# A hybrid diffusion step on one core: attention's K, V and Q loads on ScalarE's DMA queue with third Q and gate buffers, and DRAM scratch laid out by chunk and by head

## The chip, the cores and the metric

The kernel runs on one core of a Trainium2 chip. The metric is device microseconds from launch to end. The program is one launch that computes two layers and the final norm.

## What is computed

The reference runs a backbone of two layers on 1024 latent tokens and 128 context tokens (model width 1024). Cut to what matters here, one layer is:

```python
u = rms_norm(x, norm1_g) * (1 + sc1) + sh1
(aq, ak, av), dl, ml, bg, co = prep_mixers(u, w_in, ...)      # one projection
a = diff_attention(rope(aq), concat(rope(ak), k_ctx), concat(av, v_ctx), lam)   # 4 heads, 2 maps each
o_d = delta_bidir(...)                                        # 4 heads, gated DeltaNet, both directions
h_m = mlstm_bidir(...)                                        # 4 heads, mLSTM, both directions
x = x + g1 * (concat(norm(a), norm(o_d)*silu(bg), sigmoid(co)*norm(h_m)) @ w_out)
x = x + g2 * swiglu(rms_norm(x, norm2_g) * (1 + sc2) + sh2)
```

Attention takes, per head, two softmax maps over nine tiles of 128 keys (eight latent, one cached) for latent queries and one tile for context queries, and subtracts the second map times lambda from the first.

## The kernel before

All data is float32; a dense product is split into high and low parts and takes three matmuls (`mm3`, L189 to L191). A layer has four stages: the input projection (w_in), in which column blocks of the projection are made and written to scratch in DRAM; the mixers (the rest of prep2, attention, and the two chunked recurrences with merge); the output projection (w_out); and the FFN. In the profiled execution layer 0's w_in ends at about 547 us and its mixers at about 950; layer 1's mixers run from about 2427 to 2830.

The scratch in DRAM is made by open_s (L411): BT (conv outputs q, k, v of DeltaNet, transposed), CQK (mLSTM's q and k), QD and KD (attention's q and k in two parts), VD (attention's values), BC (gates), ND and RD (DeltaNet's prepared chunks). Stores into it: blk_b L727 (BT), blk_c L746 (CQK), tok_cols L560 (BC) and L565 (VD), attn_consts L924 (cached values into VD). Loads out of it: prep1 L754 (`cv` from BT) and L756 (`c` from CQK), delta_step L1062 (`qk` from BT), mlstm_step L1149 (`cq` from CQK), merge L1188 (`bc` from BC).

prep2 works on a pair of chunks: it loads `w` from ND (L851), solves a triangular system with small matmuls (tile `px`, L879 to L909, 32x32 and 64x64), with copies on ScalarE between them (`X`, L861; `T6`, L864), and stores `X` to RD (L911). Some calls of prep2 are left when w_in ends, and run beside the first attention blocks.

attention (from L1215) loops over 4 heads. Per head it loads two K tiles (L1228, 640 KB each, read as 4 groups of 32 rows of 5120 B, pool of 3 buffers), one V tile (L1231, 640 KB, 2 buffers), and for each of five blocks of queries a Q tile in two DMAs (L1236, 2 buffers). Per 128 queries: scores `s` on TensorE (L1250), scaling and running maximum on VectorE (L1251), exp on ScalarE (L1256), the difference of the maps on VectorE and GpSimd, transposes (L1277), copies `wt` out of PSUM on ScalarE or VectorE (L1280), the product `o` with V (L1284), its square sum and scaling on ScalarE (L1287, L1292).

```python
k = self.t(at, [P, NT + P], "K", 3, F32R)
nc.sync.dma_start(k.bitcast(F32), S["KD"][h // 2].rearrange("l p r t -> (l p) r t")[:, r:r + 32, :])
V = self.t(at, [P, 10, 128], "V", 2)
nc.sync.dma_start(V, S["VD"][:, :, 128 * h:128 * h + 128].rearrange("s p e -> p s e"))
q = self.t(at, [P, 2, 2, 256], "Q", 2, F32R)
```

The order of instructions on each engine and DMA queue is set when the program is built: the scheduler simulates the program's engines and buffers and writes down one order for each. On the chip each engine runs its own order strictly, and a DMA that is issued by SyncE (SP) or ScalarE (ACT) is one instruction of that engine: if it has to wait, what stands behind it on that engine waits too. Beside the data it depends on, each DMA of these two queues waits for the completion semaphore that it takes (there are eight, DMAHW0 to DMAHW7, given out in turn), and so for the DMA that held it last.

Of the kernel before, what the change touches and what calls it, by code (L numbers as in the profile page):

```python
# [9 lines left out]
F32 = mybir.dt.float32  # L10
# [7 lines left out]
P = 128  # L18
# [52 lines left out]
class Kern:  # L71
# [362 lines left out]
    def open_s(self, l):  # L434

        S = self.S = {}
        dt = lambda n, shape: self.dr.tile(shape, F32, name=f"{n}{l}")
        S["BT"] = dt("BT", [P, 6, CVO])
        S["CQK"] = dt("CQK", [P, 4, NT])
        S["V1"] = dt("V1", [NCH, P, H, 65])  # L440
        S["BC"] = dt("BC", [NCH, P, 512])
        S["QD"] = dt("QD", [8, 2, 64, NT])
        S["KD"] = dt("KD", [2, 2, 2, P, NT + P])
        S["VD"] = dt("VD", [10, P, 512])
        S["ND"] = dt("ND", [2, NCH, P, H, P])
        S["RD"] = dt("RD", [2, NCH, P, 1024])
        S["GR"] = dt("GR", [2, 16, NT])
        S["VK"] = dt("VK", [NCH, P, 768])
        S["RM"] = dt("RM", [2, NCH, P, 768])
        S["CAT"] = dt("CAT", [KB, P, NT])  # L450
        ed, pe = ExitStack(), ExitStack()
        self.dn = ed.enter_context(self.pool("psdn", PSUM))
        self.pp = pe.enter_context(self.pool("pspp", PSUM))
        return ed, pe
# [69 lines left out]
    def tok_cols(self, l, u, i, pr):  # L524
# [17 lines left out]
        for tt in range(NCH):  # L542
# [13 lines left out]
            else:  # L556
# [8 lines left out]
                nc.sync.dma_start(S["VD"][tt if tt < 8 else 9, :, off:off + 256], v)  # L565
            yield

# [137 lines left out]
    def blk_b(self, l, b, u):  # L705
# [21 lines left out]
        nc.sync.dma_start(S["BT"][:, b, :], a)  # L727
# [8 lines left out]
    def blk_c(self, l, b, u):  # L736
        nc, S, pr = self.nc, self.S, self.pr
        w = self.load_w(self.A["w_st"][l, 6 + b])
        bias = self.p(l, "bst")[:, 6 + b:7 + b]
        for g in range(NG):  # L740
            ps = self.ps(self.dn, "dn", 2)
            self.block(ps[:, :GW], w, u[g])
            o = self.t(pr, [P, GW], "gw", GB)
            nc.scalar.activation(o, ps[:, :GW], AF.Identity, bias=bias)
            c = slice(GW * g, GW * g + GW)
            nc.sync.dma_start(S["CQK"][:, b, c], o)  # L746

    def prep1(self, l, c, c1):

        nc, S, pr, pp = self.nc, self.S, self.ch, self.pp  # L750
        o = slice(cpos(c), cpos(c) + 128)
        oc = slice(128 * c, 128 * c + 128)
        q6 = self.t(self.cv, [P, CVW], "cv", 4)[:, :768].rearrange("p (a t) -> p a t", t=128)
        nc.sync.dma_start(q6, S["BT"][:, :, o])  # L754
        c4 = self.t(c1, [P, 4, 128], "c4", 1)
        nc.sync.dma_start(c4, S["CQK"][:, :, oc])  # L756
# [157 lines left out]
    def attn_consts(self, l):  # L914
# [6 lines left out]
        for i in range(2):  # L921
            cv = self.t(pr, [P, GW], "gw", GB)[:, :256]
            nc.sync.dma_start(cv, A["cv"][l][:, 256 * i:256 * i + 256])
            nc.sync.dma_start(S["VD"][8, :, 256 * i:256 * i + 256], cv)  # L924
# [121 lines left out]
    def delta_step(self, l, cs, S0, S1, seen):  # L1046
# [12 lines left out]
        if S0 is not None:  # L1059
            qk = self.t(sc, [P, 2, 4, 128], "qk", 2)  # L1060
            for d in range(2):
                nc.sync.dma_start(qk[:, d], S["BT"][:, 0:4, cpos(cs[d]):cpos(cs[d]) + 128])  # L1062
# [63 lines left out]
    def mlstm_step(self, l, cs, C0, C1, seen):  # L1126
# [4 lines left out]
        for d in range(2):  # L1131
# [15 lines left out]
            if C0 is not None:  # L1147
                cq = self.t(sc, [P, 2, 128], "cq", 3)
                nc.sync.dma_start(cq, S["CQK"][:, 0:2, 128 * c:128 * c + 128])  # L1149
# [34 lines left out]
    def merge(self, l, c):  # L1184

        nc, S, sc, pz = self.nc, self.S, self.sc, self.pz
        bc = self.t(sc, [P, 512], "bc", 2)
# [23 lines left out]
    def attention(self, l):  # L1211
# [11 lines left out]
        for h in range(H):  # L1223
            K = []
            for m in range(2):
                k = self.t(at, [P, NT + P], "K", 3, F32R)
                r = 64 * (h % 2) + 32 * m
                nc.sync.dma_start(k.bitcast(F32), S["KD"][h // 2].rearrange("l p r t -> (l p) r t")[:, r:r + 32, :])  # L1228
                K.append(k)
            V = self.t(at, [P, 10, 128], "V", 2)  # L1230
            nc.sync.dma_start(V, S["VD"][:, :, 128 * h:128 * h + 128].rearrange("s p e -> p s e"))  # L1231
            for q0 in range(0, NT, 256):
                nq = min(256, NT - q0)
                q = self.t(at, [P, 2, 2, 256], "Q", 2, F32R)
                for hh in range(2):
                    nc.sync.dma_start(q[64 * hh:64 * hh + 64, :, :, :nq].bitcast(F32), S["QD"][2 * h:2 * h + 2, :, :, q0:q0 + nq].rearrange("m l p t -> p m l t"))  # L1236
# [317 lines left out]
```

## Time and profile before

| | us |
|---|---|
| median of 3 runs | 3792.27 (3789.85 to 3796.47) |
| profiled execution | 3797.68 |
| its span, first to last instruction | 3795.9 |
| TensorE busy | 3540.6 (93%) |
| VectorE busy | 2295.8 (60%) |
| ScalarE busy | 1136.6 (30%) |
| GpSimd busy | 654.4 (17%) |
| mean granted TensorE clock | 0.954 of full speed |

The page gives shares of busy time over the whole span. The views that follow it cut the span into stretches, list one engine's instructions in time order with what ended each idle time, and sum what an engine waited for. SPq and ACTq are the DMA-issuing instructions of SyncE and ScalarE: a long one is an issue that stood waiting.

### The profile page before, as it was taken

What the parts mean: (1) busy time and instruction counts of PE and PEld (TensorE: products, weight loads), DVE (VectorE), ACT (ScalarE), POOL (GpSimd) and SP (SyncE); (2) the same over time, 40 slices, a digit from 0 to 9 for tenths busy, and PEclk for the clock granted to TensorE, in tenths of its full rate; (3) what the DMA queues carried; (4) which work ended last, traced back from release to release, by engine and by line L of the source; (5) the groups of instructions that cost most, each with busy time, mean ns of one, the idle gap of its engine ahead of it and who ended that gap; (6) DMA issues with size and microseconds to landing.
All of it is one profiled execution on the core that took longest, in us unless ns stands there. A gap on an engine that the chain in (4) does not pass through costs nothing. (4 is left out here: it accounts for less than half of the span.)

```text
span 3795.9 us, 59415 instructions
## 1 busy us (share of the span) xinstructions
PE 3540.6 (93%) x22770; PEld 3369.8 (89%) x22770; DVE 2295.8 (60%) x5361; ACT 1136.6 (30%) x2383; POOL 654.4 (17%) x903
## 2 busy tenths in 40 slices
PE   7999978997899999999999997898789999999998
PEld 6997777886899999999989877788778999999997
DVE  7896677787455566654485567477775434333435
ACT  5323315445241111111243431244553311111111
POOL 2014232355020000000020324034632000000001
PEclk8999988999999999999999999889999999999999
DMA  5377624774212222221133663467542111111111
GB/s 215 128 247 234 217 78 124 225 214 132 92 59 84 78 81 81 95 78 48 59 110 99 221 230 97 132 175 205 137 140 66 34 39 41 49 40 39 51 45 56
DMA packets 277091, 434.13 MB, mean 114 GB/s; under 512 B 24648, under 2 KB 186504, under 8 KB 276552
## 3 DMA queue, kind: packets, MB, share of 16 engines
q1 hardware_dynamic: 247576, 324.29, 27.3%
q10 hardware_dynamic: 29232, 106.05, 8.7%
q8 instruction: 180, 2.95, 0.3%
q14 instruction: 103, 0.84, 0.1%
HBM read 315.85 MB, written 114.39 MB: 113 GB/s over the span
## 5 line engine op out<-in xcount | busy, mean ns | idle before, releaser
L362 DVE SCALAR_TENSOR_TENSOR x<-pd,mod,x 128x256 f32<-128x256 f32 (+1 forms) x832 | 405.2, 514 | 597.5 <-PE pd L191 596.3
L183 ACT CAST wh<-wr 128x1024 fp32r<-128x1024 f32 (+1 forms) x219 | 229.1, 1047 | 880.3 <-PE pu L190 462.2
L184 DVE TENSOR_TENSOR wl<-wr,wh 128x1024 fp32r<-128x1024 f32 (+1 forms) x219 | 267.6, 1228 | 173.6 <-ACT wh L183 173.1
L189 PE MATMUL pd<-hh,wh 128*128 128x384 f32 x1056 | 358.8, 340 | 7.3 <-DVE x L362 5.1
L189 PE MATMUL pg<-uh,wh 128*128 128x384 f32 x1056 | 357.2, 338 | 2.6 <-ACT uh L342 2.6
L190 PE MATMUL pg<-ul,wh 128*128 128x384 f32 x1056 | 357.9, 339 | 1.4 <-DVE ul L347 1.4
L299 POOL TENSOR_TENSOR nacc<-nacc,nsq 128x384 f32<-128x384 f32 x48 | 52.1, 1086 | 1769.6 <-issue 1572.7
L190 PE MATMUL pu<-ul,wh 128*128 128x384 f32 x1056 | 355.7, 337 | 0.0
L189 PE MATMUL pu<-uh,wh 128*128 128x384 f32 x1056 | 355.6, 337 | 0.0
L190 PE MATMUL pd<-hl,wh 128*128 128x384 f32 x1056 | 354.9, 336 | 0.0
L191 PE MATMUL pg<-uh,wl 128*128 128x384 f32 x1056 | 354.7, 339 | 0.0
L191 PE MATMUL pd<-hh,wl 128*128 128x384 f32 x1056 | 353.7, 336 | 0.0
L191 PE MATMUL pu<-uh,wl 128*128 128x384 f32 x1056 | 350.7, 337 | 0.0
L189 PE MATMUL dn<-uh,wh 128*128 128x384 f32 x864 | 300.1, 347 | 5.8 <-ACT gw L956 4.4
L190 PE MATMUL dn<-ul,wh 128*128 128x384 f32 x864 | 299.0, 346 | 0.0
L191 PE MATMUL dn<-uh,wl 128*128 128x384 f32 x864 | 298.2, 345 | 0.1
L1250 PE MATMUL s<-K,Q 128*128 128x384 f32 (+1 forms) x800 | 226.3, 393 | 58.6 <-DVE e L1251 23.7
L1251 DVE TENSOR_SCALAR_CACHE_REDUCE e<-s 128x384 f32<-128x384 f32 (+1 forms) x400 | 209.8, 539 | 67.8 <-PE s L1250 64.6
L189 PEld LDWEIGHTS pd<-hh,wh 128*128 128x128 f32 x1056 | 198.4, 188 | 18.6 <-issue 7.7
L189 PE MATMUL dn<-wh,uh 128*128 128x256 f32 (+1 forms) x624 | 186.2, 298 | 26.2 <-DVE gw L558 19.8
L1250 PEld LDWEIGHTS s<-K,Q 128*128 128x128 f32 x800 | 138.3, 207 | 78.8 <-DVE e L1251 39.0
L189 PEld LDWEIGHTS pg<-uh,wh 128*128 128x128 f32 x1056 | 199.5, 189 | 4.5 <-ACT uh L342 2.8
(354 smaller groups left out, 8221.6 us busy)
## 6 DMA issues: line engine op xcount, KB each, us to landing
wr<-in_w_gu_dram ACTq DMA_DIRECT2D x88, 512.0 KB
aw<-in_w_mod_dram SPq DMA_DIRECT2D x96, 256.0 KB
wr<-in_w_dn_dram ACTq DMA_DIRECT2D x44, 512.0 KB
wr<-in_w_st_dram ACTq DMA_DIRECT2D x36, 512.0 KB
rd<-RD SPq DMA_DIRECT2D x36, 512.0 KB
aw<-in_w_mod_dram SPq DMA_DIRECT2D x32, 512.0 KB
Q<-QD SPq DMA_DIRECT2D x64, 256.0 KB
RM<-em SPq DMA_DIRECT2D x36, 384.0 KB
```

Of the source, the lines that this page charges most:

```text
L183: nc.scalar.copy(hi, r)
L184: (eng or nc.vector).tensor_tensor(out=lo, in0=r, in1=hi.bitcast(F32), op=ALU.subtract)
L189: mm(out, lhsT=wh, rhs=xh, start=start, stop=False)
L190: mm(out, lhsT=wh, rhs=xl, start=False, stop=False)
L191: mm(out, lhsT=wl, rhs=xh, start=False, stop=stop)
L299: (nc.gpsimd if k in PST else nc.vector).tensor_tensor(out=self.acc[g], in0=self.acc[g], in1=s, op=ALU.add)
L362: nc.vector.scalar_tensor_tensor(out=x[g][k][:, lo:hi], in0=ps[:, lo:hi], scalar=gate[:, k, cnd:cnd + 1], in1=x[g][k][:, lo:hi], op0=ALU.m ...
L1250: nc.tensor.matmul(p[:, :w], lhsT=q[:, m, hl, 128 * j:128 * j + 128], rhs=K[m][:, 128 * ks[0]:128 * ks[0] + w], start=hl == 0, stop=hl == 1)
L1251: nc.vector.tensor_scalar(out=e[:, GW * i:GW * i + w], in0=p[:, :w], scalar1=0.125, scalar2=None, op0=ALU.mult, op1=ALU.max, accum_out=mx[ ...
```

## The change

The 16 K loads, 8 V loads and 80 Q DMAs of attention are issued by ScalarE where SyncE issued them. Q has three buffers where it had two, merge's `bc` too; K keeps three and V two. BT and CQK are laid out by chunk (a chunk's rows are contiguous for each partition), VD by head. A load of `cv`, `c`, `qk`, `cq` or V then reads one contiguous run per partition (3072 B for `cv`, 5120 B for V, where it read six or ten runs of 512 B); the stores to BT, CQK and VD write runs of 512 B, and BT's is split in two DMAs.

```diff
@@ -435,13 +435,13 @@
 
         S = self.S = {}
         dt = lambda n, shape: self.dr.tile(shape, F32, name=f"{n}{l}")
-        S["BT"] = dt("BT", [P, 6, CVO])
-        S["CQK"] = dt("CQK", [P, 4, NT])
+        S["BT"] = dt("BT", [NCH, P, 6, P])
+        S["CQK"] = dt("CQK", [NCH, P, 4, P])
         S["V1"] = dt("V1", [NCH, P, H, 65])
         S["BC"] = dt("BC", [NCH, P, 512])
         S["QD"] = dt("QD", [8, 2, 64, NT])
         S["KD"] = dt("KD", [2, 2, 2, P, NT + P])
-        S["VD"] = dt("VD", [10, P, 512])
+        S["VD"] = dt("VD", [H, P, 10, P])
         S["ND"] = dt("ND", [2, NCH, P, H, P])
         S["RD"] = dt("RD", [2, NCH, P, 1024])
         S["GR"] = dt("GR", [2, 16, NT])
@@ -562,8 +562,12 @@
                     continue
                 if tt == 8:
                     nc.sync.dma_start(self.O["v"][l, :, off:off + 256], v)
-                nc.sync.dma_start(S["VD"][tt if tt < 8 else 9, :, off:off + 256], v)
+                self.put_v(i - 1, tt if tt < 8 else 9, v)
             yield
+
+    def put_v(self, half, s, v):
+
+        self.nc.sync.dma_start(self.S["VD"][2 * half:2 * half + 2, :, s, :].rearrange("h p e -> p h e"), v.rearrange("p (h e) -> p h e", h=2))
 
     def softplus(self, pool, z, shape):
 
@@ -724,7 +728,8 @@
             nc.vector.scalar_tensor_tensor(out=a, in0=raw[:, j:j + CVO], scalar=cw[:, 5 * b + j:5 * b + j + 1], in1=a, op0=ALU.mult, op1=ALU.add)
         nc.scalar.activation(raw[:, :CVO], a, AF.Tanh)
         nc.vector.scalar_tensor_tensor(out=a, in0=raw[:, :CVO], scalar=1.0, in1=a, op0=ALU.add, op1=ALU.mult)
-        nc.sync.dma_start(S["BT"][:, b, :], a)
+        nc.sync.dma_start(S["BT"][0:8, :, b, :].rearrange("c p t -> p c t"), a[:, :NL].rearrange("p (c t) -> p c t", t=P))
+        nc.sync.dma_start(S["BT"][8, :, b, :], a[:, cpos(8):cpos(8) + P])
         if b < 4:
             sq = raw
             nc.scalar.activation(sq[:, :CVO], a, AF.Square)
@@ -742,18 +747,16 @@
             self.block(ps[:, :GW], w, u[g])
             o = self.t(pr, [P, GW], "gw", GB)
             nc.scalar.activation(o, ps[:, :GW], AF.Identity, bias=bias)
-            c = slice(GW * g, GW * g + GW)
-            nc.sync.dma_start(S["CQK"][:, b, c], o)
+            nc.sync.dma_start(S["CQK"][3 * g:3 * g + 3, :, b, :].rearrange("c p t -> p c t"), o.rearrange("p (c t) -> p c t", t=P))
 
     def prep1(self, l, c, c1):
 
         nc, S, pr, pp = self.nc, self.S, self.ch, self.pp
-        o = slice(cpos(c), cpos(c) + 128)
         oc = slice(128 * c, 128 * c + 128)
         q6 = self.t(self.cv, [P, CVW], "cv", 4)[:, :768].rearrange("p (a t) -> p a t", t=128)
-        nc.sync.dma_start(q6, S["BT"][:, :, o])
+        nc.sync.dma_start(q6, S["BT"][c])
         c4 = self.t(c1, [P, 4, 128], "c4", 1)
-        nc.sync.dma_start(c4, S["CQK"][:, :, oc])
+        nc.sync.dma_start(c4, S["CQK"][c])
         cq, ck = c4[:, 0:2], c4[:, 2:4]
 
         b4 = lambda a, w=64: a[:, :, None].to_broadcast([P, H, w])
@@ -921,7 +924,7 @@
         for i in range(2):
             cv = self.t(pr, [P, GW], "gw", GB)[:, :256]
             nc.sync.dma_start(cv, A["cv"][l][:, 256 * i:256 * i + 256])
-            nc.sync.dma_start(S["VD"][8, :, 256 * i:256 * i + 256], cv)
+            self.put_v(i, 8, cv)
         self.nlam = self.nlams[l]
 
     def put(self, dst, src, w):
@@ -1059,7 +1062,7 @@
         if S0 is not None:
             qk = self.t(sc, [P, 2, 4, 128], "qk", 2)
             for d in range(2):
-                nc.sync.dma_start(qk[:, d], S["BT"][:, 0:4, cpos(cs[d]):cpos(cs[d]) + 128])
+                nc.sync.dma_start(qk[:, d], S["BT"][cs[d], :, 0:4, :])
             pk = self.ps(pz, "z", 2)
             for d in range(2):
                 for p in range(2):
@@ -1146,7 +1149,7 @@
             nd = hv(nf)
             if C0 is not None:
                 cq = self.t(sc, [P, 2, 128], "cq", 3)
-                nc.sync.dma_start(cq, S["CQK"][:, 0:2, 128 * c:128 * c + 128])
+                nc.sync.dma_start(cq, S["CQK"][c, :, 0:2, :])
                 pq = self.ps(pz, "y", 1)
                 for p in range(2):
                     nc.tensor.matmul(pq[:, 130 * p:130 * p + 130], lhsT=cq[:, p, :], rhs=C0[:, d, p, :], start=True, stop=True)
@@ -1184,7 +1187,7 @@
     def merge(self, l, c):
 
         nc, S, sc, pz = self.nc, self.S, self.sc, self.pz
-        bc = self.t(sc, [P, 512], "bc", 2)
+        bc = self.t(sc, [P, 512], "bc", 3)
         nc.sync.dma_start(bc, S["BC"][c])
         th = self.t(sc, [P, 512], "bh", 2)
         nc.scalar.activation(th, bc, AF.Tanh, scale=0.5)
@@ -1225,15 +1228,15 @@
             for m in range(2):
                 k = self.t(at, [P, NT + P], "K", 3, F32R)
                 r = 64 * (h % 2) + 32 * m
-                nc.sync.dma_start(k.bitcast(F32), S["KD"][h // 2].rearrange("l p r t -> (l p) r t")[:, r:r + 32, :])
+                nc.scalar.dma_start(k.bitcast(F32), S["KD"][h // 2].rearrange("l p r t -> (l p) r t")[:, r:r + 32, :])
                 K.append(k)
             V = self.t(at, [P, 10, 128], "V", 2)
-            nc.sync.dma_start(V, S["VD"][:, :, 128 * h:128 * h + 128].rearrange("s p e -> p s e"))
+            nc.scalar.dma_start(V, S["VD"][h])
             for q0 in range(0, NT, 256):
                 nq = min(256, NT - q0)
-                q = self.t(at, [P, 2, 2, 256], "Q", 2, F32R)
+                q = self.t(at, [P, 2, 2, 256], "Q", 3, F32R)
                 for hh in range(2):
-                    nc.sync.dma_start(q[64 * hh:64 * hh + 64, :, :, :nq].bitcast(F32), S["QD"][2 * h:2 * h + 2, :, :, q0:q0 + nq].rearrange("m l p t -> p m l t"))
+                    nc.scalar.dma_start(q[64 * hh:64 * hh + 64, :, :, :nq].bitcast(F32), S["QD"][2 * h:2 * h + 2, :, :, q0:q0 + nq].rearrange("m l p t -> p m l t"))
                 ctx = q0 >= NL
                 kt = [9] if ctx else list(range(9))
                 groups = [kt] if ctx else [kt[0:3], kt[3:6], kt[6:9]]
```

The scheduler orders the whole program anew. The number of instructions on TensorE, VectorE and GpSimd is unchanged. Two places follow, both in layer 0 where w_in ends and attention begins.

SyncE's queue, before, from head 0's second K load on (w2 is prep2's `w`, RD the store of its `X`; the semaphore that a DMA waits for stands in brackets):

```order
L1228 DMA K_1519_7844<-KD0_122 128x1x1280 [waits DMAHW2_49]
L1231 DMA V_1520_7846<-VD0_123 128x10x128 [waits DMAHW3_49]
L1236 DMA Q_1521_7848<-QD0_121 64x4x256 [waits DMAHW4_49]
L1236 DMA Q_1521_7848<-QD0_121 64x4x256 [waits DMAHW5_49]
L851 DMA w2_755_3823<-ND0_124 128x512 [waits DMAHW6_49,PE_49]
L851 DMA w2_756_3831<-ND0_124 128x512 [waits DMAHW7_49,PE_49]
L1236 DMA Q_1575_8016<-QD0_121 64x4x256 [waits DMAHW0_49]
```

There w2_755 and w2_756 stand behind the K, V and Q loads, and w2_756 also waits for the semaphore that K_1518 took (DMAHW7).

ScalarE's queue, after, from head 0's first K load on, waits shown in the same way:

```order
L1231 DMA K_1518_7848<-KD0_122 128x1x1280 [waits DMAHW7_49,PE_49]
L867 COPY T6_681_3296<-cv_684_3369 32x4x32 [waits PE_49,Activation_49]
L867 COPY T6_681_3296<-cv_684_3369 32x4x32 [waits Activation_49]
L1231 DMA K_1519_7850<-KD0_122 128x1x1280 [waits DMAHW1_49]
L1234 DMA V_1520_7852<-VD0_123 128x1280 [waits DMAHW6_49,DMAHW3_49]
L1239 DMA Q_1521_7854<-QD0_121 64x4x256 [waits DMAHW5_49]
L1239 DMA Q_1521_7854<-QD0_121 64x4x256 [waits DMAHW7_49]
L867 COPY T6_680_3295<-cv_682_3303 32x4x32 [waits PE_49,Activation_49]
L867 COPY T6_680_3295<-cv_682_3303 32x4x32 [waits Activation_49]
L867 COPY T6_681_3296<-cv_684_3369 32x4x32 [waits PE_49,Activation_49]
L867 COPY T6_681_3296<-cv_684_3369 32x4x32 [waits Activation_49]
L1239 DMA Q_1575_8022<-QD0_121 64x4x256 [waits DMAHW1_49]
```

The loads left SyncE's queue, where prep2's w2 loads stood behind them, and now stand between ScalarE's copies for prep2. The second half of Q_1521 waits for the semaphore that K_1518 holds (DMAHW7), and Q_1575 for K_1519's (DMAHW1), with copies behind both.

TensorE, before, around the first scores `s`:

```order
L901 MATMUL px_749_3795<-T6_680_3289,w2_733_3715 64x64 x4
L901 MATMUL px_751_3802<-T6_681_3290,w2_734_3723 64x64 x4
L1250 MATMUL s_1525_7854<-K_1518_7842,Q_1521_7848 128x384 x2
L1250 MATMUL s_1526_7858<-K_1518_7842,Q_1521_7848 128x384 x2
L909 MATMUL px_753_3809<-X2_676_3285,qq_750_3800 64x64 x4
L909 MATMUL px_754_3816<-X2_678_3287,qq_752_3807 64x64 x4
L879 MATMUL px_757_3839<-cv_682_3297,w2_755_3823 32x32 x4
```

Here the first scores stand right behind px_751, ahead of px_757, the next call of prep2.

TensorE, after, from the same px_749 on:

```order
L904 MATMUL px_749_3801<-T6_680_3295,w2_733_3721 64x64 x4
L904 MATMUL px_751_3808<-T6_681_3296,w2_734_3729 64x64 x4
L912 MATMUL px_753_3815<-X2_676_3291,qq_750_3806 64x64 x4
L912 MATMUL px_754_3822<-X2_678_3293,qq_752_3813 64x64 x4
L882 MATMUL px_757_3845<-cv_682_3303,w2_755_3829 32x32 x4
L882 MATMUL px_759_3852<-cv_684_3369,w2_756_3837 32x32 x4
...
L904 MATMUL px_771_3909<-T6_680_3295,w2_755_3829 64x64 x4
L904 MATMUL px_773_3916<-T6_681_3296,w2_756_3837 64x64 x4
L1253 MATMUL s_1525_7860<-K_1518_7848,Q_1521_7854 128x384 x2
```

The first scores stand one call of prep2 later on TensorE: px_757 to px_773, which need w2_755 and w2_756, now come ahead of them.

## Rows read from the trace of the kernel before

**Rows 1.** Stretches of the mixers: busy us (instructions) per engine, clock, DMA share, GB/s
```profile
547.00:950.00 403.00, 343.59 (x3005) 310.19 (x3004) 304.88 (x1024) 201.66 (x490) 168.73 (x212) 0.90 0.59 172
...
2427.00:2830.00 403.00, 336.87 (x2652) 307.90 (x2649) 297.01 (x979) 188.76 (x443) 162.88 (x207) 0.87 0.61 171
```

**Rows 2.** Waits of PE from 547 to 2890 us: total, times, longest (us)
```profile
PE s L1250 <- DVE e L1251: 23.7, 33, 5.9
PE s L1250 <- DMA Q<-QD: 17.4, 4, 7.9
PE s L1250 <- DMA K<-KD: 16.8, 3, 9.0
PE px L879 <- DMA w<-ND: 13.2, 3, 8.6
...
PE t L1277 <- ACT wt L1280: 12.1, 7, 4.3
...
PE o L1219 <- ACT fin L1292: 9.3, 9, 3.2
```

**Rows 3.** Timeline of SP's DMA issues, layer 0: start, us, operation
```profile
547.01 0.59 SPq L1228 DMA_DIRECT2D K<-KD  x1
...
550.04 14.62 SPq L1236 DMA_DIRECT2D Q<-QD  x2
...
573.50 9.39 SPq L851 DMA_DIRECT2D w<-ND  x2
```

**Rows 4.** Timeline of SP's DMA issues, layer 1
```profile
2425.36 0.57 SPq L1228 DMA_DIRECT2D K<-KD  x1
...
2431.37 12.13 SPq L851 DMA_DIRECT2D w<-ND  x1
```

**Rows 5.** Timeline of PE, layer 0: the first scores, and the idle before them
```profile
572.86 1.62 PE L1250 MATMUL s<-K,Q 128*128 128x384 f32 x4 [9.04 <-DMA K<-KD]
```

**Rows 6.** Timeline of PE, layer 1: the first scores
```profile
2455.87 1.33 PE L1250 MATMUL s<-K,Q 128*128 128x384 f32 x3
```

**Rows 7.** Short stretches of layer 0, columns as in rows 1
```profile
552.00:554.00 2.00, 2.00 (x21) 1.71 (x20) 1.16 (x3) 1.13 (x4) 0.00 (x0) 0.50 1.17 181
560.00:564.00 4.00, 2.47 (x32) 2.22 (x32) 1.93 (x7) 1.74 (x6) 0.00 (x0) 0.50 0.26 106
571.00:572.00 1.00, 0.00 (x0) 0.00 (x0) 0.00 (x0) 0.00 (x0) 0.00 (x0) 0.50 1.05 322
```

**Rows 8.** Stretches at the start of layer 0's mixers
```profile
555.00:573.00 18.00, 4.86 (x81) 4.50 (x82) 3.26 (x11) 2.36 (x8) 0.00 (x0) 0.50 0.60 163
573.00:601.00 28.00, 24.73 (x192) 20.29 (x193) 17.84 (x60) 13.21 (x34) 3.87 (x4) 0.53 0.52 145
601.00:612.00 11.00, 11.00 (x142) 9.56 (x141) 9.94 (x37) 7.69 (x19) 2.65 (x3) 1.00 0.23 73
```

**Rows 9.** Stretches at the start of layer 1's mixers
```profile
2435.00:2456.00 21.00, 8.37 (x126) 7.36 (x123) 5.15 (x17) 3.42 (x12) 0.00 (x0) 0.50 0.73 177
2456.00:2489.00 33.00, 29.41 (x226) 24.52 (x227) 20.84 (x70) 13.33 (x35) 4.20 (x4) 0.53 0.37 110
```

**Rows 10.** Waits of SP's DMA issues from 545 to 1010 us
```profile
SPq L1236 <- PE s L1250: 23.0, 7, 7.7
...
SPq L1231 <- PE o L1284: 14.0, 1, 14.0
...
SPq L1236 <- PE t L1277: 11.3, 5, 4.5
```

**Rows 11.** Issues by tile, whole span: ns min/median/max, first and last start
```profile
L1236 SPq DMA_DIRECT2D Q<-QD x80: 573/598/13964, 550.0 to 2805.1; - x80
...
L1228 SPq DMA_DIRECT2D K<-KD x16: 536/557/2634, 547.0 to 2741.2; - x16
...
L1231 SPq DMA_DIRECT2D V<-VD x8: 371/375/715, 549.3 to 2681.0; - x8
...
L754 SPq DMA_DIRECT2D cv<-BT x18: 523/562/2600, 218.2 to 2176.1; - x18
...
L756 SPq DMA_DIRECT2D c<-CQK x18: 518/611/2849, 299.5 to 2235.8; - x18
```

## The prediction

> **What bounds the kernel now.** I read first the table of stretches. In both mixer stages TensorE is busy for 343.59 and 336.87 us of 403, so some 59 and 66 us are idle there [rows 1]; the diff changes no matmul, so what it can win is idle time of TensorE in these stages, or time at a low clock. The other stages are left at what they cost now. Second, TensorE's waits: the largest are for VectorE's `e` (23.7 us), which the change does not touch; then Q loads (17.4 in 4 waits), K loads (16.8 in 3, the longest 9.0), and prep2's `w` loads (13.2, the longest 8.6) [rows 2]. The last three sum to 47.4 us and are all transfers out of scratch. Third, the timelines tell where they come from. Layer 0's first K is issued at 547.01; SyncE then stands 14.62 us in its two Q issues, and later 9.39 us in two `w` issues [rows 3]. In layer 1 K goes out at 2425.36 and a `w` issue stands 12.13 us [rows 4]. The first scores come at 572.86, 25.9 us after K's issue, with TensorE idle for the 9.04 us before them [rows 5]; in layer 1 at 2455.87, 30.5 us after [rows 6]. So at the start of each attention one queue carries K, V, Q and prep2's `w`, and whatever stands behind the K pair is late, prep2 too.
>
> Why K is slow shows in a short stretch. From 560 to 564 the DMA engines' share is 0.26, about 4 of 16, at 106 GB/s [rows 7], and what is then left to move is K. One K of 655,360 bytes at that rate takes 6.2 us, the pair 12.4. The change leaves K's layout as it was.
>
> **The change, part by part.**
>
> *Start of attention.* TensorE is busy 4.86 us of the 18 from 555 to 573 [rows 8] and 8.37 of the 21 from 2435 to 2456 [rows 9]: 13.1 and 12.6 us idle. This is the most that the move can win there. With K, V and Q on ScalarE's queue, SyncE can issue `w` at once, and TensorE has a whole call of prep2 ahead of the first scores. What is late next is K itself: the second half of the first Q waits for the first K's semaphore, so scores can't start before 6.2 us plus that Q's own transfer, and the second K needs 12.4. I expect the first scores 12 to 16 us after K's issue, where they take 25.9 and 30.5. Of each idle time I take 9 us as won and some 4 as left for K: -9 and -9. Bounds: 0 (the copies that prep2 needs stand as late on ScalarE as `w` stood on SyncE) and -25.7 (all of it).
>
> *Q loads in mid-attention.* SyncE stands 23.0 + 11.3 us in layer 0 for a free Q buffer [rows 10], and TensorE waits 17.4 us for Q in both layers [rows 2]. A third buffer lets a load go out one block earlier, and DeltaNet's and mLSTM's loads no longer stand behind it. I take 10 of the 17.4, since some of these waits are the transfer itself. Bounds: 0 and -17.4.
>
> *K in mid-attention.* Of 16.8 us the 9.0 belong to the start; 7.8 are left. K still has three buffers and the same slow transfer: 0, bounds -7.8 and +7.8 (K now queues behind ScalarE's work).
>
> *ScalarE's new work.* 80 Q issues at 0.598 us, 16 K at 0.557 and 8 V at 0.375 [rows 11] are 47.8 + 8.9 + 3.0 = 59.7 us. ScalarE is busy for 201.66 + 188.76 = 390.4 us of the two mixer stages [rows 1], so it has room. How much is exposed I judge by what TensorE waits for ScalarE today: 12.1 + 9.3 us [rows 2] for 390.4 us of work, 5.5%, which makes 3.3 us of 59.7. An issue ahead of an exp also delays the chain through VectorE to the transposes, so I take +6. Bounds: 0 (more work can't help) and +30 (half of it on the path).
>
> *Layout.* The 18 `cv` and 18 `c` loads take SyncE 0.562 and 0.611 us of issue now [rows 11]; with one run per partition they can hardly take more than V's present 0.375, so SyncE saves 36 x 0.2 = 7 us or so; the split of BT's store adds 12 issues of like size, 4 to 5 us. Both lie beside w_in's dense matmuls. V's ten runs per partition become one. I take 0; if all that is saved or added were on the path, -7 or +5. When the dense matmuls are gone, at the start of attention, V's transfer counts, and it lies within the bounds above. Here row and rule part. At full DMA share 552 to 554, where V's 512-byte runs go beside K, moves 181 GB/s; at 571 to 572, with Q and `w` in longer runs, a share of 1.05 moves 322 [rows 7]. By the rows, then, V's runs are slow to move. The Trainium skill ("DMA: Bandwidth & Descriptors", section "Specifications") says that line rate needs transfers of 512 B or more, so by it the ten runs were good already and the layout wins nothing; the sum stays the same by either.
>
> *Third `bc` buffer.* It frees SyncE of a wait for `merge`, and TensorE waits for nothing of merge in [rows 2]: 0.
>
> The sum is -9 -9 -10 +6 = -22 us. The profiled execution took 3797.68 us for a span of 3795.9, 5.4 above the median of the runs shown, so it becomes 3775.7, and the median 3792.27 becomes **3770.3**, my forecast. For this case alone the range is 3755 to 3788.
>
> **The rivals.**
>
> *A: ScalarE becomes the queue that stands.* SyncE's standing for Q buffers, 34.3 us in layer 0 [rows 10] and taken as the same in layer 1, 68.6 in all, moves to ScalarE, and behind it stand exp, the `wt` copies and `fin`, all on the way to the next matmuls. So do the waits for K's semaphores in front of prep2's copies. At half exposed, 34 us stand against -9 -9 -10 +6: 3792.27 + 34 - 22 = **3804**. It decides once more than 22/68.6, a third of the old standing, is met by ScalarE. For it: an exp that is late stops everything, and the new orders were made with simulated times. Against it: with a third buffer an issue finds its buffer free more often, and ScalarE is idle for half of these stages. Chance 0.20.
>
> *B: the queue was not what was late.* K moves on 4 engines as before, V and Q fall due with it, the eight semaphores are shared by both queues, so SyncE's later DMAs still wait for K. Then the change does not do what it says at the start: both -9 fall away, and -10 +6 leaves -4: **3788**. For it: at 560 to 564 nothing but K's four engines had work, and an issue that stands may just show that. Against it: SyncE's `w` loads were late for no need of K. Beside it stands the Trainium skill ("DMA: Bandwidth & Descriptors", section "Issuing engines are not separate DMA queues"): the engines that issue share the same 16 DMA engines, and a second issuer saves only the time it takes to issue. By that rule this would be the outcome; the trace agrees that issues are short (0.6 us), but shows them standing for 14.62. Chance 0.18.
>
> *C: the clock stays up.* From 573 to 601 and from 2456 to 2489 TensorE is busy 24.73 and 29.41 us at a granted clock of 0.53 [rows 8, 9], the lower level (1.2 GHz); it is back at 1.00 from 601 on. If the idle ahead of these stretches went and the clock with it stayed at 2.4 GHz, up to 24.73 x 0.47 + 29.41 x 0.47 = 25 us more would go: 3770 - 25 = **3745**. Against it: the clock is 0.50 already at 552 to 554, where TensorE is busy all of the time with prep2's small matmuls [rows 7], before the idle time begins, and prep2's matmuls come ahead of the scores in the new order still. Chance 0.10.
>
> **How the numbers follow.** The forecast's case gets 0.52, since both of its large terms rest on waits seen in full; A 0.20, B 0.18, C 0.10. A measurement of this kernel can tell about 0.2% from no change, 7.6 us: faster is below 3784.7, slower above 3799.9. Faster: nine tenths of the main case (0.47) and C, 0.57. Same: the rest of the main case and B, 0.23. Slower: A, 0.20. The range must take in the main case, B, and the nearer halves of A and C: 3742 to 3805. That leaves A's far half and a little of C outside.
>
> **What the profile after would show.** Right: the first scores 12 to 16 us after K's issue and no SyncE issue above 5 us around it; TensorE's wait for `w` near 0 and its wait for Q below 8 us; the mixer stages 9 to 13 us shorter each, with w_in and the FFNs unchanged. ScalarE's own DMA issues would sum to about 60 us, of which few stand over 2 us. Wrong by A: ACTq issues of 3 to 10 us with exp behind them, and TensorE's waits for `e`, `wt` or `fin` grown by over 20 us. Wrong by B: the first scores still 25 us after K's issue, with TensorE waiting for K. Wrong by C: granted clock near 1 where 0.53 stands. If the FFN or w_in stretches change by more than 5 us, the reordering as such has done what no step here has.

## The result, and the profile after

The changed kernel takes 3835.86 us (median of 4 runs, 3833.01 to 3843.54) against 3793.6 before (4 runs): a ratio of 1.0112, 95% interval 1.0096 to 1.0127. It is 42 us slower where 22 us faster was forecast, and outside the range.

The page of the changed kernel (busy us, share of the span, instructions): TensorE has the same 22770 instructions; the span grew by 38.4 us. The last line is ScalarE's queue (q10), which the loads moved to.

```profile
span 3834.3 us, 59430 instructions
...
PE 3555.2 (93%) x22770; PEld 3385.2 (88%) x22770; DVE 2295.5 (60%) x5361; ACT 1135.7 (30%) x2383; POOL 659.3 (17%) x903
...
q1 hardware_dynamic: 202264, 289.65, 23.2%
q10 hardware_dynamic: 54256, 140.66, 12.0%
```

Where the 38.4 us lie is read by cutting both spans at the same places in the program: the last dense matmul of w_in, the first scores `s`, the first matmul of w_out behind the mixers, the end of the FFN, and so on into layer 1. The kernel before, cut there (start:end, length, then busy us per engine, clock, DMA share, GB/s):

```profile
0.00:547.00 547.00, 497.82 (x3066) 452.17 (x3066) 420.93 (x818) 191.11 (x404) 124.28 (x205) 0.93 0.56 188
547.00:573.00 26.00, 12.30 (x218) 11.15 (x218) 8.94 (x28) 4.72 (x16) 0.00 (x0) 0.59 0.64 161
573.00:954.00 381.00, 331.29 (x2788) 299.04 (x2788) 295.94 (x996) 197.65 (x476) 168.73 (x212) 0.92 0.59 174
...
1857.00:2428.00 571.00, 534.02 (x3669) 493.30 (x3668) 361.11 (x741) 186.76 (x429) 125.59 (x205) 0.96 0.43 140
2428.00:2456.00 28.00, 14.39 (x256) 12.90 (x253) 10.41 (x34) 5.40 (x19) 0.00 (x0) 0.58 0.73 171
2456.00:2937.00 481.00, 422.36 (x2954) 392.81 (x2954) 342.37 (x1056) 215.26 (x489) 181.38 (x225) 0.91 0.51 147
```

The changed kernel, cut at the same places:

```profile
0.00:565.00 565.00, 507.31 (x3162) 461.03 (x3162) 422.90 (x830) 193.05 (x414) 126.15 (x205) 0.92 0.55 183
565.00:595.00 30.00, 14.43 (x236) 12.59 (x234) 9.79 (x30) 1.77 (x6) 0.00 (x0) 0.61 0.63 184
595.00:998.00 403.00, 337.67 (x2676) 305.83 (x2676) 297.07 (x982) 198.13 (x476) 169.08 (x212) 0.89 0.55 161
...
1900.00:2470.00 570.00, 534.93 (x3662) 494.66 (x3661) 360.01 (x739) 186.80 (x427) 125.07 (x205) 0.96 0.43 140
2470.00:2502.00 32.00, 15.43 (x252) 13.72 (x245) 10.76 (x34) 3.31 (x12) 0.00 (x0) 0.54 0.65 163
2502.00:2976.00 474.00, 418.02 (x2971) 390.79 (x2972) 339.33 (x1057) 217.75 (x498) 184.45 (x225) 0.93 0.49 148
```

Line against line: w_in of layer 0 is 18 us longer, the start of its attention 4, the rest of its mixers 22. In layer 1 w_in is 1 shorter, the start 4 longer, and what follows up to the FFN 7 shorter. Two things stand out. Almost all of the loss is in layer 0, although both layers have the same new transfers. And 18 us of it are gone before the first K load is issued, in a stage in which K, V and Q don't occur.

ScalarE's timeline at the start of layer 0's attention, of the changed kernel (start, us, operation, idle before it and its releaser):

```profile
565.16 1.12 ACTq L1231 DMA_DIRECT2D K<-KD  x1
...
567.85 12.91 ACTq L1239 DMA_DIRECT2D Q<-QD  x2
580.87 1.25 ACT L867 COPY T<-cv 32x128 f32<-32x128 f32 x4 [13.87 <-DMA K<-KD]
589.37 6.00 ACTq L1239 DMA_DIRECT2D Q<-QD  x4
595.42 0.30 ACT L864 COPY X<-Nd 32x128 f32<-32x128 f32 x1 [13.29 <-DMA Q<-QD]
```

The second half of the first Q stands until K has landed, and prep2's copies stand behind it for 13.87 us. On TensorE the first scores come 29.7 us after K's issue, and wait for Q:

```profile
594.91 1.62 PE L1253 MATMUL s<-K,Q 128*128 128x384 f32 x4 [9.25 <-DMA Q<-QD]
```

Before, it was 25.9 us, and the row names K [rows 5]. That name is wrong: the view goes by the semaphore of Q's first half, which the next head's K had just taken over. By the increments of the semaphores in the trace, the first K had landed at 559.84 and the second at 568.38, and Q's second half landed at 572.77, just ahead of the scores. So in both kernels the first scores wait for Q. TensorE's waits from 565 to 2960 us of the changed kernel (total, times, longest), which answer to [rows 2]:

```profile
PE s L1253 <- DMA K<-KD: 31.3, 6, 7.7
PE s L1253 <- DMA Q<-QD: 20.8, 2, 11.5
PE s L1253 <- DVE e L1254: 20.8, 29, 1.8
...
PE o L1222 <- ACT fin L1295: 12.6, 7, 5.3
...
PE t L1280 <- ACT wt L1283: 10.9, 12, 1.6
```

The four waits for Q of before are gone from mid-attention: the two that are left are the two starts. K's waits in mid-attention went from 7.8 us in 2 (the 16.8 in 3 of [rows 2] less the one at the start) to 31.3 in 6.

SyncE has given up these loads but still waits for them. Of the waits of its issues from 545 to 3000 us in the changed kernel, these are the ones that K ends; they are loads of DeltaNet's and mLSTM's steps (L1018 to L1065, L1137, L1141), which need no K:

```profile
SPq L1054 <- DMA K<-KD: 19.8, 3, 12.0
SPq L1137 <- DMA K<-KD: 10.6, 1, 10.6
SPq L1065 <- DMA K<-KD: 10.4, 1, 10.4
SPq L1055 <- DMA K<-KD: 9.8, 1, 9.8
...
SPq L1018 <- DMA K<-KD: 9.3, 1, 9.3
SPq L1141 <- DMA K<-KD: 8.0, 1, 8.0
```

They sum to 67.9 us; the same rows of the kernel before sum to 19.7. What joins them to K is the completion semaphore that both take in turn.

### The profile page after: what moved, and what is told of

It reads as the page before. It is cut to its first block, busy times and chain, and to the rows that moved or that the text cites. A ratio compares the mean times of both kernels' runs of the same rounds, so it can differ in the third digit from the quotient of the medians.

```text
span 3834.3 us, 59430 instructions
## 1 busy us (share of the span) xinstructions
PE 3555.2 (93%) x22770; PEld 3385.2 (88%) x22770; DVE 2295.5 (60%) x5361; ACT 1135.7 (30%) x2383; POOL 659.3 (17%) x903
## 4 chain that ended last, share of the span: by engine, by line
PE 74%; DVE 11%; DMA 10%; issue 2%; ACT 1%; POOL 1%; SPq 0%; ACTq 0%; DVEq 0%; POOLq 0%
PE pd L189 6%; PE pd L190 6%; PE pd L191 6%; PE pg L191 5%; PE pu L190 5%; PE pu L191 5%; PE pu L189 5%; PE pg L190 5%; PE pg L189 5%; PE dn L190 4%; PE dn L189 4%; PE dn L191 4%; DMA K<-KD 3%; PE s L1253 2%; PE o L1287 2%
## 5 line engine op out<-in xcount | busy, mean ns | idle before, releaser
L1253 PE MATMUL s<-K,Q 128*128 128x384 f32 (+1 forms) x800 | 229.7, 396 | 73.5 <-DMA K<-KD 31.3
```

The costliest lines, as they stand in the source:

```text
L1253: nc.tensor.matmul(p[:, :w], lhsT=q[:, m, hl, 128 * j:128 * j + 128], rhs=K[m][:, 128 * ks[0]:128 * ks[0] + w], start=hl == 0, stop=hl == 1)
```

## The experiments

**First: which part costs.** Theory 1 put the loss on ScalarE's queue, theory 2 on the layouts with the order that comes with them, rival 3 on reordering by chance.

*The layouts alone* (loads on SyncE, buffers as before):

```diff
+        S["BT"] = dt("BT", [NCH, P, 6, P])
+        S["CQK"] = dt("CQK", [NCH, P, 4, P])
+        S["VD"] = dt("VD", [H, P, 10, P])
...
```

> The kernel before with the three layouts alone (BT, CQK by chunk, VD by head; loads on SyncE, Q and gate buffers 2). Theory 1 (the queue: ScalarE stands at Q loads behind K's semaphores): the loss is not here, 3785 to 3800 us. Theory 2 (the layouts, and the new order that the scheduler makes of them, cost layer 0's w_in its 18 us): w_in of layer 0 ends at 560 to 568 us, not at 547, and the time is 3805 to 3825. Rival 3 (each edit reorders the program and the time moves by chance): any value, and stages after layer 0's w_in differ from both kernels by over 10 us.

Measured: 3827.29 us, ratio 1.0086 (1.007 to 1.0101); w_in of layer 0 ends at 564.4. That is theory 2, 2 us above its range.

*The queue and the buffers alone*, old layouts:

```diff
-                nc.sync.dma_start(k.bitcast(F32), S["KD"]...
+                nc.scalar.dma_start(k.bitcast(F32), S["KD"]...
-            q = ... "Q", 2
+            q = ... "Q", 3
...
```

> The kernel before with K, V and Q on ScalarE and third Q and gate buffers, old layouts. Theory 1: layer 0's w_in ends at 547 as before, the first scores come 28 us or more after K's issue, the mixers grow by 15 to 25 us in all, 3805 to 3820 us. Theory 2: 3770 to 3795, the same as or faster than before. Rival 3: as for the layouts alone.

Measured: 3788.24 us, ratio 0.9983 (0.9971 to 0.9995). w_in ends at 548.4. The first scores come 30.3 us after K's issue, as theory 1 said (though the Q issue that stands there, for 16.3 us, does so with its semaphore free), but the start is only 4 us longer, and layer 1's mixers give 8 back.

*The buffers alone*, on SyncE:

```diff
-            q = ... "Q", 2
+            q = ... "Q", 3
-        bc = self.t(sc, [P, 512], "bc", 2)
+        bc = self.t(sc, [P, 512], "bc", 3)
```

> The kernel before with third Q and gate buffers alone. Theories 1 and 2: SyncE's standing for Q buffers shrinks, -10 to 0 us, 3782 to 3793. Rival 3: moves by over 10 us either way.

Measured: 3801.82 us, ratio 1.0015 (0.9999 to 1.0031): no gain, and above the 3782 to 3793 that theories 1 and 2 had here. From the first scores to w_out layer 0 took 394.7 us (381.4 before) and layer 1 up to the FFN 475.3 (481.3). A buffer more moves single stages by 6 to 13 us both ways.

*The changed kernel with K, V, Q back on SyncE*:

```diff
-                nc.scalar.dma_start(k.bitcast(F32), ...
+                nc.sync.dma_start(k.bitcast(F32), ...
...
```

> The changed kernel with K, V and Q back on SyncE (layouts and third buffers stay). Theory 1: 15 to 25 us faster than the changed kernel, 3810 to 3820, with the first scores within 26 us of K's issue. Theory 2: about as slow in layer 0's w_in as the changed kernel (it ends at 560 to 568), 3805 to 3825. Rival 3: differs from the sum of the layouts alone and the buffers alone by over 10 us.

Measured: 3815.6 us, ratio 1.0055 (1.0038 to 1.0072), with w_in ending at 565.5; theories 1 and 2 both allowed this time. So on top of the layouts the queue costs 20 us (3835.86 less 3815.6), while on the old layouts it saves 14 (3801.82 less 3788.24). Nor do the layouts (+32) and the buffers (+7) add up to what they cost together (+20). This is no sum of parts: rival 3 is alive within the mixers. But w_in's 18 us go with the layouts every time.

**Second: the transfers of the layouts, or their order?** By two counts of layer 0's order on TensorE the kernels fall into two groups. In the kernel before, 398 dense products (of three matmuls each) stand ahead of the first chunk of prep1, and 52 matmuls of prep2 ahead of w_in's last dense one. In the changed kernel it is 386 and 100. (A trace counts each of prep2's float32 matmuls twice: 104 and 200.) Splitting BT's store alone gives the second order, with the old layout:

```diff
-        nc.sync.dma_start(S["BT"][:, b, :], a)
+        nc.sync.dma_start(S["BT"][:, b, 0:NL], a[:, :NL])
+        nc.sync.dma_start(S["BT"][:, b, cpos(8):cpos(8) + P], a[:, cpos(8):cpos(8) + P])
```

> The kernel before with one edit: BT's store in two DMAs (latent columns, context columns), into the old layout; no layout, queue or buffer is changed. The scheduler gives every engine the order that it gives with BT's new layout. Theory 2a (the extra DMA makes the scheduler reorder w_in, and the new order is what costs): layer 0's w_in ends at 562 to 567 us and the time is 3810 to 3830. Theory 2b (the transfers of the new layouts cost, not the order): 547 and 3790 to 3800.

Measured: 3827.13 us, ratio 1.0092 (1.0074 to 1.011). One more store per block, with no new layout, queue or buffer, costs as much as all three layouts. Its stretches (w_in of layer 0, the mixers from the first scores on, w_in of layer 1):

```profile
0.00:568.00 568.00, 508.81 (x3161) 462.22 (x3162) 423.12 (x830) 193.14 (x414) 125.64 (x205) 0.92 0.54 182
...
596.00:991.00 395.00, 330.71 (x2668) 299.73 (x2667) 292.83 (x981) 194.73 (x464) 167.47 (x212) 0.89 0.57 166
...
1889.00:2460.00 571.00, 534.43 (x3662) 493.70 (x3660) 360.51 (x739) 186.87 (x431) 125.26 (x205) 0.96 0.43 140
```

Layer 1's w_in issues the same six extra stores and takes 571 us, as before. By the names in the traces, TensorE's order there is one and the same, but for a few neighbours that change places, in all sixteen kernels of this document. In layer 0's w_in it differs: the eight kernels that leave BT alone have one order, and the six that split its store another. So the store's transfer costs nothing where the order is kept, and layer 0's order is what is left. No kernel has that order with BT untouched.

*BT's layout* (same order on every engine as the split store):

```diff
-        nc.sync.dma_start(S["BT"][:, b, :], a)
+        nc.sync.dma_start(S["BT"][0:8, :, b, :]...
+        nc.sync.dma_start(S["BT"][8, :, b, :]...
-        nc.sync.dma_start(q6, S["BT"][:, :, o])
+        nc.sync.dma_start(q6, S["BT"][c])
```

> The kernel before with BT by chunk alone, store in two DMAs; the same order on each engine as with the store split in the old layout. Theory 2a: within 6 us of that kernel, 3810 to 3830. Theory 2b: 10 to 30 us slower than it.

Measured: 3829.39 us, ratio 1.0095 (1.0079 to 1.0112), 2 us from the split store. At a fixed order the layout itself moves nothing that these runs can tell.

*CQK's layout alone* (order of before on every engine):

```diff
-            nc.sync.dma_start(S["CQK"][:, b, c], o)
+            nc.sync.dma_start(S["CQK"][3 * g:3 * g + 3, :, b, :]...
-        nc.sync.dma_start(c4, S["CQK"][:, :, oc])
+        nc.sync.dma_start(c4, S["CQK"][c])
```

> The kernel before with CQK by chunk alone; the order of every engine is that of the kernel before. Theory 2a: 3788 to 3798, no difference. Theory 2b: 3 to 10 us slower, in both w_in stages.

Measured: 3792.35 us, ratio 0.9995 (0.9985 to 1.0005). The same.

*The whole change with one store for BT*:

```diff
-        S["BT"] = dt("BT", [NCH, P, 6, P])
+        S["BT"] = dt("BT", [NCH, P, 6, 132])
-        nc.sync.dma_start(S["BT"][0:8, ...
-        nc.sync.dma_start(S["BT"][8, ...
+        nc.sync.dma_start(S["BT"][:, :, b, :]..., ov)
...
```

> The whole change, but BT is stored in one DMA: rows of 132 columns per chunk that overlap by 4, so that the context chunk lies in the ninth; prep1 reads one run of 3168 B per partition. The number of DMAs is that of before, and TensorE's order stays far nearer to it. Theory 2a: layer 0's w_in ends at 546 to 550 us and the time is 3775 to 3795, 40 us or more under the changed kernel. Theory 2b: 3815 to 3840, as the changed kernel.

Measured: 3830.67 us, ratio 1.0097 (1.0082 to 1.0112), w_in ending at 565.6. A miss, and what was expected of the order was wrong: it too has 100 matmuls of prep2 ahead, with prep1 at 391. By the traces it is a third order of its own, alike in these two counts and in what it costs. So the extra store is one way into such an order, not the only one. BT in these rows alone, one store, the rest as before:

```diff
-        S["BT"] = dt("BT", [P, 6, CVO])
+        S["BT"] = dt("BT", [NCH, P, 6, 132])
-        nc.sync.dma_start(S["BT"][:, b, :], a)
+        nc.sync.dma_start(S["BT"][:, :, b, :]..., ov)
...
```

> The kernel before with BT alone in rows of 132 columns, one store, one run per cv load; number of DMAs, queues and other layouts as before; 100 rows of prep2 ahead of the last dense matmul. Order theory: layer 0's w_in ends at 563 to 568 us, 3815 to 3832, with layer 1's w_in, which has the same transfers and an order like before's, within 3 us of before. If the extra store of the split versions was what cost: 547 us and 3788 to 3798.

Measured: 3824.18 us, ratio 1.0083 (1.0052 to 1.0114); w_in of layer 0 ends at 567.5, and layer 1's takes 571.6 (571.2 before). This third order, without the extra store, costs the same.

*The whole change but for BT* (order of before in w_in):

```diff
-        S["BT"] = dt("BT", [NCH, P, 6, P])
+        S["BT"] = dt("BT", [P, 6, CVO])
...
```

> The whole change but for BT, which keeps its old layout and its one store: K, V, Q on ScalarE, third buffers, CQK and VD in the new layouts. In its order layer 0 has 52 rows of prep2 ahead of the last dense matmul of w_in, as the kernel before; the changed kernel, the split store and the one-store version have 100. Order theory (the order with 100 is what costs): w_in of layer 0 ends at 546 to 549 us, 3778 to 3795, about the run with the queue and buffers alone (3788). Rival (new layouts and the queue together cost, whatever the order): 3805 to 3835.

Measured: 3788.16 us, ratio 0.9979 (0.9966 to 0.9992); w_in ends at 543.5. Everything that was asked for except BT's layout is 6 us faster than before, and 48 faster than with it.

**Third: K.** In the profile before, K moved on about 4 of 16 DMA engines [rows 7]. Each K load in four DMAs of 32 rows, on the kernel before:

```diff
-                nc.sync.dma_start(k.bitcast(F32), S["KD"][h // 2].rearrange("l p r t -> (l p) r t")[:, r:r + 32, :])
+                kd = S["KD"][h // 2].rearrange("l p r t -> (l p) r t")
+                for g in range(4):
+                    nc.sync.dma_start(k[32 * g:32 * g + 32].bitcast(F32), kd[g, r:r + 32, :])
```

> The kernel before with each K load in four DMAs of 32 rows, on SyncE, nothing else changed. If K's running on 4 of 16 DMA engines is what holds the first scores: they come 12 to 18 us after K's first issue (25.9 and 30.5 before), 8 to 12 us of idle time go in each layer, 3772 to 3785 us. If the transfers share the engines anyway and the queue is full: 22 us or more after K's issue, 3788 to 3800.

Measured: 3741.65 us, ratio 0.9866 (0.9847 to 0.9886): 53 us, where the starts alone were to give 16 to 24. The first scores come 18.4 us after K's first issue. The start of layer 0's attention, and layer 1's mixers from the first scores on:

```profile
548.21:566.48 18.27, 15.84 (x272) 14.31 (x273) 11.30 (x35) 7.09 (x24) 0.00 (x0) 0.62 1.00 252
...
2424.03:2878.11 454.08, 411.02 (x2931) 383.86 (x2931) 342.62 (x1052) 216.36 (x485) 184.54 (x225) 0.94 0.53 154
```

The two profiled executions are 59 us apart, and 27 of that lie in the last stretch (481.3 before). The order of the mixers is new here too: 272 matmuls stand between w_in and the first scores where it was 217.

*The same on the version with BT as before* (ScalarE's queue):

```diff
-                nc.scalar.dma_start(k.bitcast(F32), ...
+                for g in range(4):
+                    nc.scalar.dma_start(k[32 * g:32 * g + 32].bitcast(F32), kd[g, r:r + 32, :])
```

> The version with BT as before (K, V, Q on ScalarE, third buffers, CQK and VD by chunk and head) with each K load in four DMAs. ScalarE then stands less at the Q loads behind K's semaphores: its issues near the start stand under 5 us (12.91 in the changed kernel), first scores 12 to 18 us after K's issue, 3765 to 3782 us. If ScalarE's standing does not come from K's slow landing: as without the split, 3778 to 3795.

Measured: 3733.46 us (3730.43 to 3734.97), ratio 0.9839 (0.9823 to 0.9856), the fastest of all and 32 us under its range. Its starts in layer 0 and 1, and between them layer 0's mixers:

```profile
546.00:564.00 18.00, 15.94 (x276) 14.25 (x274) 11.30 (x35) 7.08 (x24) 0.00 (x0) 0.64 0.96 265
564.00:929.00 365.00, 330.54 (x2733) 298.91 (x2733) 297.02 (x990) 195.86 (x468) 169.85 (x212) 0.93 0.62 180
...
2398.00:2417.00 19.00, 17.31 (x282) 15.77 (x282) 12.00 (x38) 4.72 (x16) 0.00 (x0) 0.58 0.88 266
```

The DMA share at the start is 0.96 at 265 GB/s, where it was 0.64 at 161 before. TensorE is busy 15.94 of 18 us, and the row for K is gone from its waits, in mid-attention too; for Q this is left (547 to 2890 us):

```profile
PE s L1256 <- DMA Q<-QD: 1.4, 1, 1.4
```

SyncE's waits that K ends sum to 24.9 us here, 67.9 in the changed kernel. What part of the gain is the faster landing and what the new order that comes with it, no run tells apart; but the split wins in each of three pairs of kernels, 53, 55 and (below) 78 us.

*K on SyncE, V and Q on ScalarE* (BT as before, K whole):

```diff
-                nc.scalar.dma_start(k.bitcast(F32), ...
+                nc.sync.dma_start(k.bitcast(F32), ...
```

> The version with BT as before, but K loads stay on SyncE, V and Q on ScalarE. If the second half of Q waits for K's completion semaphore on ScalarE as it did, first scores stay 28 to 31 us after K's issue and the time equals the version with all three on ScalarE within 6 us. If the queue that K is on matters: first scores at 24 to 26 us, 4 to 8 us faster than that version.

Measured: 3805.75 us, ratio 1.0032 (1.0019 to 1.0044). A miss for both: the first scores came only 17.0 us after K's issue, but TensorE then waited for K 26.7 us and for `fin` 26.5 us in all (15.9 with all three on ScalarE). An early first score is not worth much when the K behind it is late.

*The changed kernel with K split*, by the same edit, so with the second order in w_in:

> The changed kernel with each K load in four DMAs; its order keeps 100 rows of prep2 ahead of w_in's last dense matmul. If the order itself costs in layer 0's w_in and mixers, whatever K does: w_in ends at 563 to 568 us, the time is 20 to 40 us above the split version with BT as before (3733), 3753 to 3773. If the order only cost because K's slow landing came later on top of it: 3733 to 3748.

Measured: 3758.31 us, ratio 0.991 (0.9891 to 0.9929), 25 us above the split version with BT as before; with K whole the two are 48 apart. Layer 0's w_in and its mixers:

```profile
0.00:567.00 567.00, 509.46 (x3162) 462.68 (x3162) 422.88 (x830) 193.74 (x414) 127.14 (x205) 0.92 0.54 183
...
586.00:959.00 373.00, 329.11 (x2620) 296.95 (x2618) 294.06 (x978) 191.96 (x457) 167.38 (x212) 0.91 0.58 176
```

w_in is 21 us longer than in the version with BT as before, the mixers 8, with K fast in both. So the order costs without K's slow landing, and nearly twice as much (48) with it.

## Why the prediction was wrong

**The step that failed** is the layouts: "Both lie beside w_in's dense matmuls ... I take 0; if all that is saved or added were on the path, -7 or +5." As transfers that held: CQK's layout moves nothing at a fixed order, and BT's is 2 us from the split store. But BT's edit also made the scheduler write another order for layer 0, and that was priced at nothing. That order, or the third one like it, costs 30 to 36 us in the four runs that have it without the queue and the buffers (3824 to 3829 against 3794 or 3795), 17 to 21 of it in w_in. The prediction named the sign ("If the FFN or w_in stretches change by more than 5 us, the reordering as such has done what no step here has") but gave it neither a term nor a chance. It was there to be seen: the order listings, compared over the whole of w_in and not at two places, show prep1 and prep2 moved ahead of dense matmuls.

What the order does in w_in shows in part. TensorE's waits from 300 us to the end of w_in, before:

```profile
PE pp L771 <- DMA c<-CQK: 4.3, 2, 3.8
PE dn L190 <- DVE wl L184: 3.9, 2, 3.3
...
PE pp L793 <- DVE em L775: 2.2, 3, 1.3
```

and after:

```profile
PE dn L190 <- DVE wl L184: 10.5, 2, 5.8
PE pp L796 <- DVE em L778: 8.2, 3, 5.0
PE pp L774 <- DMA c<-CQK: 6.9, 1, 6.9
```

Prep1's matmuls (`pp`) now stand earlier in TensorE's order and wait longer for their inputs, and the dense ones (`dn`) for the low part of their weights from VectorE, whose order changed too: 15 us more in these three waits, less where others shrank. By the stretches TensorE is idle 8.5 us longer in w_in (57.7 against 49.2) and busy 9.5 us longer (507.31 against 497.82), at a mean granted clock of 0.92 where it was 0.93. Of the busy time some is work that came forward: prep2's matmuls there take 8.74 us, 5.24 before; prep1's take 118.36 and took 113.55 for the same 650. Which of these follows from which was not separated.

**Start of attention, -9 and -9:** measured +4 and +2 in the run with the queue and the buffers alone, and +4 and +4 in the changed kernel. That K on 4 engines makes the start late was rightly seen, as the split shows, but the move doesn't touch it, and the new order put Q's second half behind K's semaphore. That was written down as a floor of "6.2 us plus that Q's own transfer"; it came to 29.7. The first K took 15.0 us, not 6.2, beside a V and a second K, and Q's second half, issued when it had landed (the issue ends at 580.76), another 14. Before the change, too, the first K took 12.8 us and the second 19.7. What held SyncE in the kernel before stays open: its 14.62 us in [rows 3] were nearly all the issue of Q's first half, whose semaphore had been free since 545.26, so neither K's semaphore nor a busy buffer held it.

**Q in mid-attention, -10 of 17.4:** the waits went as forecast, all of them. But K's took their place, 31.3 us in 6, where the bound was 7.8 either way: a third Q buffer brings TensorE sooner to the next K. K's loads are waited for both on TensorE and, through the semaphores, on SyncE. The run with the buffers alone shows the same: no wait for Q is left there in mid-attention, and K's are 17.8 us in 5. This term failed, though its row was in view.

**ScalarE's +6:** TensorE's waits for it (`wt`, `fin`) went from 21.4 to 23.5 us, 2.1 of the 6; the rest no run shows.

**The rivals.** Case B was right that the queue was not what was late. It gave 3788, and both runs of the queue without BT's layout measured 3788, but that they agree to the microsecond is luck: B had -10 for Q and +6 for ScalarE, and the run has +4 and +2 at the starts, -8 in layer 1's mixers and small changes elsewhere. The rule of the Trainium skill ("DMA: Bandwidth & Descriptors", section "Issuing engines are not separate DMA queues") that stood beside it agrees with these runs: with another issuer the first K landed 14.8 us after its issue (queue and buffers alone), 12.8 before, while with the split the first scores came sooner. Case A's picture, ScalarE standing behind K's semaphore with prep2's copies behind it, is in the timeline at 13.87 us; but its price rested on ScalarE standing for Q buffers, and that is not what came: in layer 0's mixers after the start, the waits of ScalarE that scores end sum to 8 us. TensorE's waits for `e`, `wt` and `fin` did not grow by the 20 us that A named either. With the old layouts the same queue takes 3788, so it isn't the cause alone; on top of the new ones 20 of the 42 us go with it, and by what path is open. Case C did not happen in layer 0: in the fastest version, where TensorE is idle for 2 of the 18 us of the start, the granted clock is 0.50 from 564 to 592, right behind it, where 0.53 stood before, so still the lower level. In layer 1 it is 0.67 from 2417 to 2450 against 0.53, and it is 0.67 in the changed kernel too (2502 to 2535), which idles as before.

**What stays open:** in layer 0's mixers the same queue move costs 14 us with the second order (389.1 to 403.3, from the first scores to w_out) and saves 12 with the first (394.7 to 382.5). Only whole orders were compared, so which placement in them does it is not known. In layer 1's mixers TensorE has one and the same order in the changed kernel, in the run with the queue and the buffers alone, and in the version with BT as before: 473.6, 473.5 and 475.8 us. So there the new layouts win and cost nothing.

## What to carry to other kernels

When a scheduler writes the order, an edit that looks local (one more store) can reorder a stage far from it, so compare the built order over all stages before costing the transfers, and give the reordering a term and a range of its own. To tell an edit's transfers from its order, run a twin that has the order without the edit, and look for the same transfers in a stage that kept its order. When a load runs at a quarter of the DMA engines' share, change the load's shape before its queue. When a few semaphores are taken in turn, the name that a view gives for what ended a wait can be the semaphore's next owner: compare the times of landing.

## What the runs showed of the hardware

A load written as 4 groups of 32 rows of 5120 B ran at a DMA share of 0.26 and 106 GB/s while little else moved [rows 7]. The same bytes as four DMAs of 32 rows each, on the same queue, brought the start of layer 0's attention from a share of 0.64 and 161 GB/s to 1.00 and 252 GB/s. With 48 DMAs more to issue, the kernel was 53 us faster.

A DMA issue can stand with its semaphore free. At the start of layer 0's attention the issue of Q's first half stood 10.4 to 16.3 us in the seven kernels where a whole K and a V in ten runs per partition were issued ahead of it, and under 1 us in the nine where V was one run per partition or K was split. What it stood for, no view shows.
